# A planned hybrid decoder layer: buffers taken in the order of the plan, with slack in the plan, on one NeuronCore

## Chip, cores and metric

One NeuronCore of a Trainium2 chip runs the whole layer. The metric is the device time of one execution in microseconds (us). The engines are TensorE (PE, with its weight loads PEld), VectorE (DVE), ScalarE (ACT), GpSimd (POOL) and SyncE (SP), which issues most of the DMAs; ACT issues the others.

## What is computed

The input x is 1024 tokens by 1024 channels. One RMS norm, one combined projection, three groups of heads, a gate for each group, one output projection, the residual and a last RMS norm:

```python
h = rms_norm(x)
p = h @ w_in                                   # columns for three groups
# RWKV-7, 8 heads of 64: a state S (64x64 per head), token after token
sa = einsum(S, -kk_t)
S  = S * w_t + sa * (kk_t * a_t) + v_t * k_t   # decay, delta rule, new value
y  = einsum(S, r_t)
# sparse attention, 4 heads of 64: three branches, summed under gates
# memory attention, 4 heads of 64, into 256 memory tokens
out = rms_norm(x + concat(rwkv, nsa, mem) * silu(gates) @ w_out)
```

## The kernel before

**The work.** Every wide projection is made three times with 128x512 products: the weights are split in a high part `wh` (ACT, line 635) and a low part `wl` (POOL or DVE, line 636) of one loaded tile `wr` (line 640, one buffer), and the normed input in two such parts `H`. A weight tile costs 48 products `pa<-H,wh` and `pa<-H,wl` and is needed by nothing else.

**RWKV** goes by four pairs of heads (hp0 to hp3 here), and then by 16 chunks of 64 tokens. DVE, ACT and POOL make the factors of a pair, PE multiplies them (`pa<-A,NP`), DVE masks the results (line 1007) and SP stores them in DRAM (`st_d`, lines 1011 to 1014). Within each chunk a triangular matrix has to be inverted. That is done for two pairs of heads at once, which is why there are two of them: **inverse 0** after hp1 and **inverse 1** after hp3. Each one

- loads the 32x32 diagonal blocks from `st_d` in an array A (line 818),
- makes 31 steps on DVE, two instructions each (lines 826 and 827, shapes of 31, 60, 87, ... elements that grow and then shrink again),
- copies the result (ACT, line 829), stores it in `md` and `nd` (lines 830, 832), loads `st_d` over A (line 839), `nd` in `S` (line 841, issued by ACT) and `md` in A (line 844),
- makes the remaining off-diagonal blocks by 32x32 products on PE (`pa<-S,A`, `pa<-A,S`), copies them (line 859), and stores the inverse in `st_d` (line 861).

The chunks load their matrices from `st_d` (line 1446). They are a chain through the state: each waits for the one before (`ch<-T,C`, `ch<-xe,C`, and ACT's copy `xe<-ch` of line 1468, once per chunk). The projections of the memory and sparse groups, their attention and the output projection have no part in this chain, and fill PE between its links.

**What sets the order.** Nothing of the order is left to chance. The stages are generators, and `flow()` runs them in a written order. Then a planner, `ordered()`, reads all instructions, estimates how long each takes, finds the dependences, ranks each instruction by how much work hangs on it (`_backward`) and plays the program once through (`_forward`): whichever instruction of an engine is ready and has the highest rank goes next. This is repeated `ROUNDS` times with the last result as the start, the best plan is kept, and each engine's instructions are chained in its order.

**Buffers.** Tiles of one tag share a few buffers. In the kernel before, tiles were given to buffers when the instructions were written, so in the written order; the planner had to keep it, and a rule in `_edges` held it there: a tile's writers may not begin before the first user of the tile before it in its tag.

Of the kernel before, what the change touches and what calls it, by code (L numbers as in the profile page):

```python
# [131 lines left out]

def _access(x):

    a = x.bass_ap
    t = a.tensor
    p = tuple((int(s), int(c)) for s, c in a.ap)
    n = 1
    for s, c in p[1:]:
        n *= c  # L140
    if type(t).__name__ != "Tile":
        return None, None, "D", p, n
    if t.space == DRAM:
# [12 lines left out]
    p0, c0 = divmod(int(a.offset), row)
    w = 1 if a.dtype == BF else 2
    key = (c0, p[1:], w)
    if key not in _MASKS:
        idx = np.array([c0])  # L160
        for s, c in p[1:]:
            idx = np.unique((idx[:, None] + np.arange(c)[None, :] * s).ravel())
        _MASKS[key] = _bits((idx[:, None] * w + np.arange(w)[None, :]).ravel())
    return t, {q: _MASKS[key] for q in range(p0 // 32, (p0 + p[0][1] - 1) // 32 + 1)}, "S", p, n


def _times(o, ins, outs):

    i, kind = o.i, o.kind
    n = max([x[4] for x in ins + outs] or [1])  # L170
    psum = any(x[2] == "P" for x in ins)
    big = sum(x[4] > 1 for x in ins)
    o.lock = False
    if o.e == "Activation":
        few = sum(x[4] == 1 for x in ins) if n > 1 else 0
        o.took = 170 + 0.84 * n + 85 * (few > 0) + 110 * (len(outs) > 1)
        o.occ = o.took - 110
    elif o.e == "DVE":
        if kind == "InstMemset":
            o.took = 60 + 0.83 * n  # L180
        elif kind == "InstTensorCopy" and not psum:
            o.took = 150 + 0.53 * n
        elif getattr(i, "is_tensor_tensor_scan", False):
            o.took = 150 + 2.1 * n
        elif kind == "InstTensorScalarPtr" and big == 1 and not psum and not getattr(i, "is_scalar_tensor_tensor", False):
            o.took = 150 + 0.5 * n
        else:
            o.took = 145 + 1.045 * n
        if kind == "InstTensorScalarPtr" and n > 64 and sum(x[4] == 1 for x in ins):
            o.took += 60  # L190
        o.occ = max(60.0, o.took - 82)
        o.lock = not psum and (kind == "InstTensorTensor" or kind == "InstTensorCopy" or getattr(i, "is_scalar_tensor_tensor", False))
    else:
        if kind == "InstMemset":
            o.took = 98 + 0.83 * n
        elif kind == "InstTensorTensor" and i.op == OP.pow:
            o.took = 380 + 157 * n
        elif kind == "InstTensorTensor":
            o.took = 165 + 2.15 * n if n < 1000 else 2600.0
        else:  # L200
            o.took = 185 + 0.5 * n
        o.occ = o.took - 42 if n > 8 else o.took + 70
        o.lock = bool(ins)


def _matmul(i):
    mov, sta = i.ins[0].bass_ap, i.ins[1].bass_ap
    n = 1
    for s, c in tuple(mov.ap)[1:]:
        n *= c  # L210
    c = 1
    for s, q in tuple(sta.ap)[1:]:
        c *= q
    r = tuple(sta.ap)[0][1]
    kind = "r" if sta.dtype == F32R else "b" if sta.dtype == BF else "t" if i.is_transpose else "f"
# [25 lines left out]
    return {"r": 180 + 0.42 * s[3], "t": 195 + 0.84 * s[3], "b": 205 + 0.42 * s[3], "f": 255 + 0.84 * s[3]}[s[0]]  # L241


def _read(instructions):
    ops = []
    for k, i in enumerate(instructions):
        kind = type(i).__name__
        if kind in ("BassTilePoolBoundary", "InstTileManualSchedule"):
            continue
        o = Op()  # L250
        o.i, o.k, o.kind, o.e = i, len(ops), kind, str(i.engine).split(".")[-1]
        ins = [_access(x) for x in i.ins if hasattr(x, "bass_ap")]
        outs = [_access(x) for x in i.outs if hasattr(x, "bass_ap")]
        o.reads, o.writes = [x[:2] for x in ins if x[0] is not None], [x[:2] for x in outs if x[0] is not None]
        o.dma, o.lock, o.shape = None, False, None
        if kind == "InstDMACopy":
            run = 1 << 30
            for t, m, w, p, n in ins + outs:
                c = 1
                for s, q in reversed(p):  # L260
                    if s != c and q != 1:
                        break
                    c *= q
                run = min(run, 4 * c)
            n = 4 * ins[0][4] * ins[0][3][0][1]
            d = min(run, 8192)
            n = max(4 * outs[0][4] * outs[0][3][0][1], 4) / d
            load = outs[0][2] == "S"
            o.dma = (330 + max(0.0, n - 256) * 0.7, 1170.0 if load else 670.0, n * (9 + d * 0.0366) / 16, 720.0 if load else 450.0)
            o.took = sum(o.dma)  # L270
            o.occ = o.dma[0] + 50 if o.e == "SP" else 200.0
        elif o.e == "PE":
            o.shape = _matmul(i)
            o.occ, o.took = _step(o.shape), _done(o.shape)
        else:
            _times(o, ins, outs)
        ops.append(o)
    return ops


def _depend(ops):
# [62 lines left out]
    return took, late  # L344


def _edges(ops, users, tags, took):

    preds = [None] * len(ops)
    for o in ops:  # L350
        preds[o.k] = {p: 0 for p in o.data}
        for p in o.same:
            preds[o.k][p] = 1
    for names in tags.values():
        for a, b in zip(names, names[1:]):
            p = users[a][0]
            for k in users[b]:
                if k != p and any(w[0].name == b for w in ops[k].writes):
                    preds[k].setdefault(p, 2)
    for t, old in took.items():  # L360

        for k in users[t]:
            if any(w[0].name == t for w in ops[k].writes):
                for p in users[old]:
                    if p != k:
                        preds[k][p] = 1 if ops[k].e == "PE" and ops[p].e == "PE" else 0

    after, head = {}, list(range(len(ops)))
    for a, b in zip(ops, ops[1:]):
        if a.e == b.e == "PE" and _mode(a.shape) == _mode(b.shape) != (128, 128) and len(block(head, a.k, after)) < BLOCK:  # L370
            after[a.k] = b.k
            head[b.k] = head[a.k]
    for k in range(len(ops)):
        h = head[k]
        if h != k:
            for p, same in preds[k].items():
                if head[p] != h:
                    preds[h][p] = min(same, preds[h].get(p, 2))
    for o in ops:
        o.preds = preds[o.k]  # L380
    return preds, after
# [56 lines left out]
def _forward(ops, preds, after, rank, phase):  # L438
# [20 lines left out]
    while done < n:  # L459
# [73 lines left out]
    return order, start, end  # L533


MARGIN = 0.0
FIRST = 250
BLOCK = 32
SWITCH = 700.0
BUFS = {"A_a": N_A, "C_a": 2, "P4_p4": N_P4, "NP_p4": N_NP, "S2_s2": N_S2, "N2_s2": N_N2, "T2_s2": N_T2, "H_h": 2, "wr_w": N_WR,  # L540
        "wl_w": 2, "wh_w": 2, "pa_ps": 6, "ch_ps": 2, "ss_small": 2, "edge_small": 2, "n8_small": 2, "ost_small": 2, "mst_small": 4,
        "cst_small": 1, "st_small": 2, "wst_small": 3, "xe_small": 1, "sgc_small": 1, "md_dram": 2, "nd_dram": 2}
ROUNDS = 10


def ordered(nc, tc, log=None):
    ops = _read(list(nc.cur_bb.bb.instructions))
    _depend(ops)
    users, tags = _tiles(ops)
    seq = list(range(len(ops)))  # L550
    best, start = None, seq
    for n in range(ROUNDS):
        took, late = _slots(users, tags, seq)
        preds, after = _edges(ops, users, tags, took)
        rank = _backward(ops, preds, start)
        rank = [r + max(0.0, FIRST - k) * 1e3 for k, r in enumerate(rank)]
        order, start, end = _forward(ops, preds, after, rank, 1100.0)
        if log is not None:
            log(n, late, end)
        if best is None or end < best[0]:  # L560
            best = end, order
        seq = sorted(range(len(ops)), key=lambda k: (start[k], k))
    end, order = best
    for e, line in order.items():
        for a, b in zip(line, line[1:]):
            tc.add_manual_dep(ops[b].i, ops[a].i.name, mybir.DependencyInfo(mybir.DependencyClass.NoSync, mybir.DependencyReason.DATA), reason="order")


def build(tc, x, mem, w_in, w_gl, w_kv, w_out, lora, pv_d, rows_d, cst_d, rope_d, w1_d, pos_d, w2_d, out):
    nc = tc.nc  # L570
    V, S, G, PE = nc.vector, nc.scalar, nc.gpsimd, nc.tensor
    ctx = ExitStack()
    with ctx:
# [1224 lines left out]
        spawn(R_O, out_proj())  # L1798
        spawn(R_P, projections())
        flow()  # L1800
        ordered(nc, tc)

# [99 lines left out]
```

## Time and profile before

| quantity | value |
|---|---|
| median of three runs | 800.5 us (799.58 to 803.46) |
| profiled execution | 801.87 us |
| its span in the trace | 800.1 us |
| its mean granted TensorE clock | 0.968 of full speed |
| PE busy | 730.0 us, 91% of the span |
| DVE, ACT, POOL busy | 531.3, 387.8, 349.4 us |

The span is what the trace shows from the first instruction to the last; the execution has 1.8 us more. PE's share of busy time is a mean over stages, and its clock has two levels, 2.4 GHz (granted 1.0) and 1.2 GHz (granted 0.5); a granted clock between them is a mean over a stretch.

### The profile page before, as it was taken

To read this page: it belongs to the slowest core of one execution; us is meant where nothing else is said; L and a number is where in the kernel's file an instruction comes from. 1 tells how busy PE (TensorE), PEld (TensorE's weight loads), DVE (VectorE), ACT (ScalarE), POOL (GpSimd) and SP (SyncE) were. 2 spreads that over 40 slices of the span, in tenths; PEclk is the share of its full clock that TensorE was granted. 3 is DMA by queue.
4 is the path that set the end of the run, shared out by engine and by line. 5 is a ranking of instruction groups with operands and counts; after the bars stand their busy time and mean duration, and the time that the engine had idled before them with its cause. 6 is when DMAs were issued, how large, how long until landed. Compare 5 with 4: busy or idle time off the path is not lost. (4 is left out here: it accounts for less than half of the span.)

```text
span 800.1 us, 15116 instructions
## 1 busy us (share of the span) xinstructions
PE 730.0 (91%) x5738; PEld 599.8 (75%) x5738; DVE 531.3 (66%) x1044; ACT 387.8 (48%) x854; POOL 349.4 (44%) x370
## 2 busy tenths in 40 slices
PE   3889999999980899898999989999998999999996
PEld 3778888888870787686886767676777889888885
DVE  5843677488994449652679875938878767776432
ACT  5553344353532024323477744544477666665531
POOL 3535528264540013122445656655334054255674
PEclk9999999999995699898999999999999999999999
DMA  8111674756469873594755585532525020121121
GB/s 336 43 54 40 161 169 107 200 142 159 119 158 189 142 197 118 128 196 164 231 164 176 186 262 180 200 120 62 157 80 151 2 79 28 54 79 54 54 86 59
DMA packets 124744, 105.67 MB, mean 132 GB/s; under 512 B 50816, under 2 KB 108544, under 8 KB 122496
## 3 DMA queue, kind: packets, MB, share of 16 engines
q1 hardware_dynamic: 108096, 95.57, 42.7%
q10 hardware_dynamic: 16576, 9.14, 4.2%
q8 instruction: 45, 0.74, 0.4%
q14 instruction: 27, 0.22, 0.1%
HBM read 68.52 MB, written 36.18 MB: 131 GB/s over the span
## 5 line engine op out<-in xcount | busy, mean ns | idle before, releaser
L610 PE MATMUL pa<-H,wh 128*128 128x512 f32 (+1 forms) x928 | 292.2, 395 | 4.6 <-DVE H L705 2.9
L610 PEld LDWEIGHTS pa<-H,wh 128*128 128x128 f32 x928 | 170.9, 191 | 40.0 <-DVE H L705 4.0
L610 PE MATMUL pa<-H,wl 128*128 128x512 f32 (+1 forms) x464 | 181.1, 391 | 0.3 <-DVE wl L636 0.3
L636 POOL TENSOR_TENSOR wl<-wr,wh 128x1024 fp32r<-128x1024 f32 x27 | 68.0, 2518 | 88.3 <-ACT wh L635 71.5
L610 PEld LDWEIGHTS pa<-H,wl 128*128 128x128 f32 x464 | 88.0, 190 | 18.2 <-DVE wl L636 0.8
L610 PE MATMUL ch<-H,C 128*128 128x512 f32 x360 | 100.6, 407 | 0.0
L610 PE MATMUL pa<-A 128*128 128x256 f32 (+4 forms) x416 | 75.1, 306 | 2.5 <-DVE A L897 2.1
L635 ACT ACTIVATE wh<-wr 128x1024 fp32r<-128x1024 f32 x32 | 33.9, 1058 | 79.2 <-PE pa L610 72.8
L610 PEld LDWEIGHTS ch<-H,C 128*128 128x128 f32 x360 | 64.0, 189 | 10.0
L610 PEld LDWEIGHTS pa<-A 128*128 128x128 f32 (+1 forms) x416 | 51.1, 173 | 8.1 <-issue 2.5
L1171 DVE TENSOR_TENSOR N<-pa,S 128x512 fp32r<-128x512 f32 (+1 forms) x76 | 44.8, 613 | 17.8 <-ACT S L1170 15.2
L1596 DVE TENSOR_REDUCE wst<-pa 128x1 f32<-128x384 f32 (+3 forms) x96 | 46.6, 514 | 12.1 <-PE pa L610 11.7
L610 PEld LDWEIGHTS ch<-T,C 128*64 128x64 f32 (+1 forms) x1008 | 35.1, 139 | 22.1 <-ACT T L1483 5.7
L610 PE MATMUL ch<-T,C 128*64 128x64 f32 (+1 forms) x1008 | 42.1, 230 | 8.8 <-DMA C<-st_d 3.1
L1170 ACT ACTIVATE S<-pa 128x512 fp32r<-128x512 f32 (+1 forms) x76 | 38.5, 542 | 16.7 <-PE pa L1636 15.9
L1493 DVE SCALAR_TENSOR_TENSOR T<-ch,gc,sgc 64x64 f32<-64x64 f32 x120 | 33.9, 283 | 9.2 <-PE ch L610 5.5
L876 ACT ACTIVATE T<-pa,pv 128x512 f32<-128x512 f32 x34 | 23.1, 679 | 32.4 <-PE pa L610 28.3
L1606 ACT ACTIVATE NP<-pa,wst 128x384 f32<-128x384 f32 (+3 forms) x52 | 29.0, 565 | 17.6 <-DVE wst L1596 11.1
L1475 POOL TENSOR_TENSOR sgc<-T,gc 64x256 f32<-64x256 f32 x30 | 20.7, 689 | 36.2 <-DVE T L1493 34.9
L1677 POOL TENSOR_TENSOR S<-S,N 128x512 f32<-128x512 f32 x8 | 10.3, 1290 | 50.3 <-DVE N L1676 22.0
L610 PE MATMUL ch<-S,A 128*128 128x256 f32 x132 | 30.9, 298 | 0.8 <-ACT S L1170 0.8
L610 PE MATMUL ch<-N,A 128*128 128x256 f32 x132 | 30.4, 297 | 1.0 <-DVE N L1171 1.0
(273 smaller groups left out, 1498.3 us busy)
## 6 DMA issues: line engine op xcount, KB each, us to landing
C<-st_d SPq DMA_DIRECT2D x16, 1024.0 KB, 5.3
wr<-in_w_in_dram SPq DMA_DIRECT2D x28, 512.0 KB, 3.8
st_d<-C SPq DMA_DIRECT2D x32, 256.0 KB, 4.7
st_d<-A SPq DMA_DIRECT2D x24, 256.0 KB, 3.7
A<-in_x_dram SPq DMA_DIRECT2D x8, 512.0 KB, 7.8
st_d<-NP SPq DMA_DIRECT2D x8, 512.0 KB, 5.3
P<-in_x_dram SPq DMA_DIRECT2D x8, 512.0 KB, 3.5
out_dram<-P SPq DMA_DIRECT2D x7, 512.0 KB, 2.7
```

The costliest lines, as they stand in the source:

```text
L610: PE.matmul(o, l, r, start=start, stop=stop, skip_group_check=True, **k)
L635: S.activation(hi, src, AF.Copy)
L636: E.tensor_sub(lo, src, hi.bitcast(F32))
L876: S.activation(t[:, 4:516], o, AF.Identity, scale=col(C_MU + idx))
L1170: S.activation(th[:, 0:w], psum_t, AF.Copy)
L1171: V.tensor_sub(tl_[:, 0:w], psum_t, th[:, 0:w].bitcast(F32))
L1475: G.tensor_mul(sgc[r], sv[r, q], gcb[r])
L1493: V.scalar_tensor_tensor(svn[r, q, hp, :], pn[r, hp, :], g1[r, hp], sgc[r, hp, :], op0=OP.mult, op1=OP.add)
L1596: V.tensor_reduce(st[:, 3 + a, hh:hh + 1], sc[:, 0:cw], axis=AX.X, op=OP.max, negate=True)
L1606: S.activation(p[:, c0:c0 + cw], sc[:, 0:cw], AF.Exp, bias=m, accum_out=acc)
L1677: G.tensor_add(bo[0], bo[0], bo[1])
```

## The change

All engine calls go through `Queues`, which writes each call down with its arguments and issues nothing. The planner reads these records in place of instructions; its formulas for durations are the same, by other names. For each tag, tiles are now sorted by their first use in the last plan (`taken`), and `_slots` gives them to buffers in that order; the rule of `_edges` that held the written order is gone. At the end, all calls are issued in the order of their planned beginnings, so that the pools hand out buffers in the plan's order. Three numbers change too: `MARGIN`, which the planner adds to every dependence between engines, from 0 to 150 ns; `BLOCK`, the largest number of small products that it keeps together, from 32 to 16; and `ROUNDS` from 10 to 30. No instruction is added, removed or given another shape: 6,994 instructions stand on both sides, one for one, in other orders.

```diff
-    for names in tags.values():
-        for a, b in zip(names, names[1:]):
-            p = users[a][0]
-            for k in users[b]:
-                if k != p and any(w[0].name == b for w in ops[k].writes):
-                    preds[k].setdefault(p, 2)
...
+class Queue:
...
+    def __getattr__(self, f):
+        def call(*args, **kw):
+            o = Op()
+            o.k, o.e, o.name, o.args, o.kw, o.call = len(self.ops), self.name, f, args, kw, getattr(self.engine, f)
+            self.ops.append(o)
+        return call
...
-MARGIN = 0.0
+MARGIN = 150.0
 FIRST = 250
-BLOCK = 32
+BLOCK = 16
...
-ROUNDS = 10
...
+ROUNDS = 30
...
     for n in range(ROUNDS):
-        took, late = _slots(users, tags, seq)
-        preds, after = _edges(ops, users, tags, took)
+        at = {k: n for n, k in enumerate(seq)}
+        taken = {t: sorted(names, key=lambda x: min(at[k] for k in users[x])) for t, names in tags.items()}
+        took, late = _slots(users, taken, seq)
+        preds, after = _edges(ops, users, took)
...
+    last = {}
+    for k in best[1]:
+        o = ops[k]
+        i = o.call(*o.args, **o.kw).ins
+        if o.e in last:
+            tc.add_manual_dep(i, last[o.e], mybir.DependencyInfo(mybir.DependencyClass.NoSync, mybir.DependencyReason.DATA), reason="order")
+        last[o.e] = i.name
...
-    nc = tc.nc
+    nc = Queues(tc.nc)
```

What this does to the order is seen in the rows of both programs. In the changed program every row has line 574, the one that issues, so rows are known by their tiles.

**PE around inverse 0.** In the kernel before its products (array `A_1462`) come directly behind two groups of 128x128 products of hp3, and the last products of hp3 (`A_1986`) come behind it, among products with the projection weights:

```order
L610 MATMUL pa_2185<-H_143,wl_2181 128x512
L1004 MATMUL ch_2434<-cst_81,NP_2216 128x128 x4
L1004 MATMUL ch_2461<-cst_81,NP_2216 128x128 x4
L610 MATMUL pa_2228<-S2_2128,A_1462 32x32 x32
L610 MATMUL pa_2322<-S2_2137,A_1462 32x32 x32
...
L610 MATMUL pa_2377<-H_143,wl_2181 128x512
...
L610 MATMUL pa_2424<-A_1986,NP_2216 128x128
...
L610 MATMUL pa_2452<-A_1986,NP_2216 128x128
```

In the changed program the array of inverse 0 is `A_336` and hp3's factors are `A_419`:

```order
L574 MATMUL pa_465<-A_419,NP_455 128x128
...
L574 MATMUL pa_469<-A_419,NP_455 128x128
...
L574 MATMUL pa_520<-H_105,wh_517 128x512
L574 MATMUL pa_459<-S2_439,A_336 32x32 x32
L574 MATMUL pa_529<-A_508,wh_528 128x256
L574 MATMUL pa_518<-H_104,wl_516 128x512
...
L574 MATMUL pa_457<-S2_438,A_336 32x32 x32
```

Inverse 0's products have moved behind the last products of hp3, and between the two now stand 137 rows, nearly all of them 128x512 products with weights. In all, 248 instructions that stood behind inverse 0's first product stand ahead of it now, 216 of them such 128x512 products. In the same way 117 have moved ahead of inverse 1's first product and 128 ahead of chunk 0's.

**DVE at the end of inverse 0.** Before, its last steps (`A_1462`) are done 18 rows ahead of the first step of inverse 1 (`A_2503`):

```order
L827 TENSOR_TENSOR A_1462<-A_1462,P4_1602 128x30x2
L826 TENSOR_TENSOR P4_1602<-A_1462 128x31
L827 TENSOR_TENSOR A_1462<-A_1462,P4_1602 128x31
...
L1007 TENSOR_TENSOR C_2210<-pa_2452,maskb_136 128x512
...
L826 TENSOR_TENSOR P4_2603<-A_2503 128x31
L827 TENSOR_TENSOR A_2503<-A_2503,P4_2603 128x31
```

In the changed program (`A_336` is inverse 0, `A_480` inverse 1):

```order
L574 TENSOR_TENSOR P4_360<-A_336 128x192
L574 TENSOR_TENSOR wl_516<-wr_515,wh_517 128x1024
L574 TENSOR_TENSOR P4_491<-A_480 128x31
L574 TENSOR_TENSOR A_336<-A_336,P4_360 128x24x8
...
L574 TENSOR_TENSOR P4_360<-A_336 128x60
L574 TENSOR_TENSOR A_480<-A_480,P4_491 128x7x25
L574 TENSOR_TENSOR A_336<-A_336,P4_360 128x30x2
L574 TENSOR_TENSOR P4_491<-A_480 128x192
L574 TENSOR_TENSOR P4_360<-A_336 128x31
L574 TENSOR_TENSOR A_480<-A_480,P4_491 128x8x24
L574 TENSOR_TENSOR A_336<-A_336,P4_360 128x31
```

The first step of inverse 1 now stands ahead of the last 15 instructions of inverse 0, and the two go on in turns: 15 of inverse 0, 16 of inverse 1 and four others from `P4_491 128x31` to the last `A_336 128x31`.

**SP behind the two inverses.** In the changed program the queue from the stores of inverse 0 on reads as follows (`wr` are weight loads, `md`, `nd` and `st_d` as above):

```order
L574 DMA md_334<-A_336 128x1024
L574 DMA nd_335<-A_336 32x1024 x2
L574 DMA A_336<-st_d_108 64x16x64 x3
L574 DMA wr_533<-in_w_in_dram 128x1024
L574 DMA A_336<-st_d_108 64x16x64
L574 DMA A_336<-md_334 32x16x32 x8
L574 DMA wr_540<-in_w_kv_dram 128x1024
...
L574 DMA A_480<-st_d_108 64x16x64 x4
L574 DMA wr_570<-in_w_kv_dram 128x1024
L574 DMA A_480<-md_478 32x16x32 x8
```

Before, inverse 0's transfers had no weight load among them, and inverse 1's had one:

```order
L830 DMA md_1460<-A_1462 128x1024
L832 DMA nd_1461<-A_1462 32x1024 x2
L839 DMA A_1462<-st_d_147 64x16x64 x4
L1050 DMA g_d_150<-T2_2170 128x512
L844 DMA A_1462<-md_1460 32x16x32 x8
...
L839 DMA A_2503<-st_d_147 64x16x64 x3
L640 DMA wr_3160<-in_w_kv_dram 128x1024
L839 DMA A_2503<-st_d_147 64x16x64
```

From the stores of inverse 0 to the first load of chunk 0, six weight loads stand in the changed queue: `wr_533`, `wr_540`, `wr_545`, `wr_559`, `wr_570`, `wr_586`.

## Rows read from the trace of the kernel before

**Rows 1.** The page: busy time of the engines, and TensorE's granted clock by slices.
```profile
PE 730.0 (91%) x5738; PEld 599.8 (75%) x5738; DVE 531.3 (66%) x1044; ACT 387.8 (48%) x854; POOL 349.4 (44%) x370
PEclk9999999999995699898999999999999999999999
```

**Rows 2.** Stretches: length, busy time and instructions of each engine, PE's granted clock, DMA share.
```profile
200.00:240.00 40.00, 37.66 (x207) 31.21 (x205) 39.13 (x66) 17.69 (x28) 20.21 (x20) 0.96 0.55 138
240.00:280.00 40.00, 18.45 (x319) 15.48 (x320) 17.93 (x37) 4.97 (x7) 0.47 (x3) 0.62 0.87 165
280.00:380.00 100.00, 91.15 (x735) 75.02 (x734) 55.78 (x117) 32.96 (x53) 23.13 (x22) 0.93 0.63 161
380.00:520.00 140.00, 133.44 (x1599) 102.30 (x1600) 108.56 (x256) 85.19 (x213) 80.57 (x89) 1.00 0.63 200
...
280.00:300.00 20.00, 20.00 (x90) 16.55 (x89) 8.41 (x20) 5.22 (x7) 2.86 (x4) 1.00 0.74 197
320.00:340.00 20.00, 16.69 (x76) 13.82 (x75) 13.26 (x34) 6.46 (x10) 3.33 (x3) 0.83 0.59 128
...
360.00:380.00 20.00, 16.08 (x156) 12.76 (x155) 4.65 (x12) 6.19 (x11) 5.91 (x4) 0.83 0.49 164
```

**Rows 3.** Timeline of PE around inverse 0: start, length, instruction, count, wait before it.
```profile
239.06 0.39 PE L610 MATMUL pa<-H,wl 128*128 128x512 f32 x1
242.35 1.06 PE L1004 MATMUL ch<-cst,NP 128*128 128x128 f32 x8 [2.90 <-DVE NP L984]
260.21 0.28 PE L610 MATMUL pa<-S,A 32*32 32x32 f32 x2 [16.80 <-DMA A<-st_d]
262.89 3.59 PE L610 MATMUL pa<-S,A 32*32 32x32 f32 x126 [2.40 <-DMA S<-nd]
...
274.74 1.16 PE L610 MATMUL pa<-A,NP 64*128 64x128 f32 x16
...
277.79 0.40 PE L610 MATMUL pa<-H,wl 128*128 128x512 f32 x1
278.11 1.16 PE L610 MATMUL pa<-A,NP 64*128 64x128 f32 x16
```

**Rows 4.** Timeline of DVE and SP's queue (SPq) ahead of inverse 0's products.
```profile
247.63 0.20 DVE L826 TENSOR_TENSOR P<-A 128x31 f32<-128x31 f32 x1
247.87 0.21 DVE L827 TENSOR_TENSOR A<-A,P 128x31 f32<-128x31 f32 x1
248.12 1.93 ACT L829 ACTIVATE A<-A 128x1024 f32<-128x1024 f32 x1 [4.01 <-DVE A L827]
...
253.74 3.97 SPq L839 DMA_DIRECT2D A<-st_d  x4
...
260.02 4.46 SPq L844 DMA_DIRECT2D A<-md  x5
```

**Rows 5.** Timeline from hp3's masks to inverse 1's first step on DVE.
```profile
279.31 1.29 DVE L1007 TENSOR_TENSOR C<-pa,maskb 128x512 f32<-128x512 f32 x2 [2.08 <-PE pa L610]
...
287.24 1.15 SPq L818 DMA_DIRECT2D A<-st_d  x2
...
294.91 0.19 DVE L826 TENSOR_TENSOR P<-A 128x31 f32<-128x31 f32 x1 [5.64 <-DMA A<-st_d]
```

**Rows 6.** Lines 827, 859 and 1468: instructions, shortest, median and longest ns, first and last start.
```profile
L827 DVE TENSOR_TENSOR A<-A,P x62: 183/363/2503, 179.1 to 330.1; 128x31 f32<-128x31 f32 x4, 128x60 f32<-128x60 f32 x4, 128x87 f32<-128x87 f32 x4, 128x112 f32<-128x112 f32 x4
...
L859 DVE COPY A<-pa x8: 679/684/691, 269.1 to 353.2; 32x512 f32<-32x512 f32 x8
...
L1468 ACT ACTIVATE xe<-ch x16: 573/597/606, 369.1 to 518.9; 128x512 f32<-128x512 f32 x16
```

**Rows 7.** Timeline of PE: first products of inverse 1 and of chunk 0.
```profile
343.01 1.20 PE L610 MATMUL pa<-S,A 32*32 32x32 f32 x64
...
367.06 1.98 PE L610 MATMUL ch<-T,C 128*64 128x64 f32 x32 [3.06 <-DMA C<-st_d]
```

**Rows 8.** The page: a weight tile's load (KB, us to landing), its split on ACT and POOL.
```profile
L636 POOL TENSOR_TENSOR wl<-wr,wh 128x1024 fp32r<-128x1024 f32 x27 | 68.0, 2518 | 88.3 <-ACT wh L635 71.5
...
L635 ACT ACTIVATE wh<-wr 128x1024 fp32r<-128x1024 f32 x32 | 33.9, 1058 | 79.2 <-PE pa L610 72.8
...
wr<-in_w_in_dram SPq DMA_DIRECT2D x28, 512.0 KB, 3.8
```

More of the change, by code (lines that the diff above doesn't have):

```diff
@@ L133, in _access @@
 def _access(x):
-    a = x.bass_ap
-    t = a.tensor
+    a, t = x, x.tensor
     p = tuple((int(s), int(c)) for s, c in a.ap)
@@ L167, in _times @@
 def _times(o, ins, outs):
-    i, kind = o.i, o.kind
+    f = o.name
     n = max([x[4] for x in ins + outs] or [1])
@@ L172, in _times @@
     big = sum(x[4] > 1 for x in ins)
+    one = sum(x[4] == 1 for x in ins)
     o.lock = False
     if o.e == "Activation":
-        few = sum(x[4] == 1 for x in ins) if n > 1 else 0
-        o.took = 170 + 0.84 * n + 85 * (few > 0) + 110 * (len(outs) > 1)
+        o.took = 170 + 0.84 * n + 85 * (one > 0 and n > 1) + 110 * (len(outs) > 1)
         o.occ = o.took - 110
     elif o.e == "DVE":
-        if kind == "InstMemset":
+        if f == "memset":
             o.took = 60 + 0.83 * n
-        elif kind == "InstTensorCopy" and not psum:
+        elif f == "tensor_copy" and not psum:
             o.took = 150 + 0.53 * n
-        elif getattr(i, "is_tensor_tensor_scan", False):
+        elif f == "tensor_tensor_scan":
             o.took = 150 + 2.1 * n
-        elif kind == "InstTensorScalarPtr" and big == 1 and not psum and not getattr(i, "is_scalar_tensor_tensor", False):
+        elif f == "tensor_scalar" and big == 1 and not psum:
             o.took = 150 + 0.5 * n
@@ L188, in _times @@
             o.took = 145 + 1.045 * n
-        if kind == "InstTensorScalarPtr" and n > 64 and sum(x[4] == 1 for x in ins):
+        if f in ("tensor_scalar", "scalar_tensor_tensor") and n > 64 and one:
             o.took += 60
         o.occ = max(60.0, o.took - 82)
-        o.lock = not psum and (kind == "InstTensorTensor" or kind == "InstTensorCopy" or getattr(i, "is_scalar_tensor_tensor", False))
+        o.lock = not psum and f in ("tensor_tensor", "tensor_mul", "tensor_sub", "tensor_add", "tensor_copy", "scalar_tensor_tensor", "tensor_tensor_scan")
     else:
-        if kind == "InstMemset":
+        if f == "memset":
             o.took = 98 + 0.83 * n
-        elif kind == "InstTensorTensor" and i.op == OP.pow:
+        elif o.kw.get("op") == OP.pow:
             o.took = 380 + 157 * n
-        elif kind == "InstTensorTensor":
+        elif f in ("tensor_mul", "tensor_sub", "tensor_add", "tensor_tensor"):
             o.took = 165 + 2.15 * n if n < 1000 else 2600.0
@@ L203, in _times, with _matmul @@
         o.lock = bool(ins)
-def _matmul(i):
-    mov, sta = i.ins[0].bass_ap, i.ins[1].bass_ap
+def _matmul(sta, mov, transposed):
     n = 1
@@ L241, in _done, with __init__, _read @@
     return {"r": 180 + 0.42 * s[3], "t": 195 + 0.84 * s[3], "b": 205 + 0.42 * s[3], "f": 255 + 0.84 * s[3]}[s[0]]
[L244 to L253, printed above, removed]
+class Queue:
+    def __init__(self, engine, name, ops):
+        self.engine, self.name, self.ops = engine, name, ops
+    def __getattr__(self, f):
[4 more added lines that the diff above has]
+        return call
+class Queues:
+    def __init__(self, nc):
+        self.ops = []
+        for n, e in (("vector", "DVE"), ("scalar", "Activation"), ("gpsimd", "Pool"), ("tensor", "PE"), ("sync", "SP")):
+            setattr(self, n, Queue(getattr(nc, n), e, self.ops))
+def _read(ops):
+    isap = lambda x: hasattr(x, "tensor") and hasattr(x, "ap")
+    for o in ops:
+        outs = [_access(x) for x in list(o.args[:1]) + [o.kw.get("accum_out")] if isap(x)]
+        ins = [_access(x) for x in list(o.args[1:]) + [v for k, v in o.kw.items() if k != "accum_out"] if isap(x)]
         o.reads, o.writes = [x[:2] for x in ins if x[0] is not None], [x[:2] for x in outs if x[0] is not None]
         o.dma, o.lock, o.shape = None, False, None
-        if kind == "InstDMACopy":
+        if o.name == "dma_start":
             run = 1 << 30
@@ L272, in _read @@
         elif o.e == "PE":
-            o.shape = _matmul(i)
+            o.shape = _matmul(o.args[2], o.args[1], True) if o.name == "transpose" else _matmul(o.args[1], o.args[2], False)
             o.occ, o.took = _step(o.shape), _done(o.shape)
@@ L344, in _slots, with _edges @@
     return took, late
-def _edges(ops, users, tags, took):
+def _edges(ops, users, took):
     preds = [None] * len(ops)
@@ L542, with ordered @@
         "cst_small": 1, "st_small": 2, "wst_small": 3, "xe_small": 1, "sgc_small": 1, "md_dram": 2, "nd_dram": 2}
-ROUNDS = 10
-def ordered(nc, tc, log=None):
-    ops = _read(list(nc.cur_bb.bb.instructions))
+ROUNDS = 30
+def ordered(tc, ops, log=None):
+    _read(ops)
     _depend(ops)
@@ L559, in ordered @@
             log(n, late, end)
+        seq = sorted(range(len(ops)), key=lambda k: (start[k], k))
         if best is None or end < best[0]:
[L561 to L566, printed above, removed]
+            best = end, seq
+    last = {}
[5 more added lines that the diff above has]
+        last[o.e] = i.name
 def build(tc, x, mem, w_in, w_gl, w_kv, w_out, lora, pv_d, rows_d, cst_d, rope_d, w1_d, pos_d, w2_d, out):
-    nc = tc.nc
+    nc = Queues(tc.nc)
     V, S, G, PE = nc.vector, nc.scalar, nc.gpsimd, nc.tensor
@@ L1800, in build @@
         flow()
-        ordered(nc, tc)
+        ordered(tc, nc.ops)
 W_OFF_NSA, W_OFF_MEM = 2176, 3084
```

4 lines of the change are left out of this document (1 added, 3 removed).

## The prediction

> **What bounds the kernel now.** I read the page first. PE is busy for 730.0 of 800.1 us and its clock is at full speed in every slice but a few in the middle [rows 1]. So PE's work sets the time, and what can be won without less work is PE's idle time and its time at half clock. The table of stretches says where both lie [rows 2]. From 280 to 300 us PE did 90 products 128x512 without a gap: 20.00 / 90 = 0.222 us each, the price of a wide product below. From 240 to 280 it is busy for 18.45 of 40 us at a mean clock of 0.62.
>
> The timeline of PE shows the hole [rows 3]. After 239.06 no product with weights stands ahead of inverse 0 any more; eight products of hp3 follow, and then PE waits 16.80 us for a load of `A<-st_d` and soon 2.40 us for `S<-nd`. It is a wait by order: the products that run from 280 to 300 need nothing of inverse 0. The chain behind the wait is DVE's last step at 247.87, ACT's copy, the stores and two rounds of loads [rows 4]: from the end of that step (248.08) to the first product at 260.21 it takes 12.1 us.
>
> What PE loses from 200 to 380 us, where the orders differ most, is this. Idle: 2.3 + 21.6 + 8.9 = 32.8 us [rows 2]. Half clock: a mean of 0.62 over 40 us is about 30 us at half, from the wait until 274; PE worked for about 11.5 of them (260.2 to 274 less 2.4), which at full clock would have taken half, so 5.7 are lost. By the same reading 0.83 over 20 us is 6.8 us at half, 3.4 lost, twice, and 0.96 over 40 us loses 1.6. Together 14.1, so **46.9 us** in all.
>
> **The change, step by step.** Writing calls down costs the device nothing: the instructions are the same, and what follows is order alone.
>
> *Inverse 0.* The products of inverse 0 now stand behind hp3's last ones, with 137 rows between: 134 wide products (29.7 us) and three groups of four 128x128, at half of 1.06 us each [rows 3], so 31.3 us of cover. What PE waits for is a chain that starts with those same hp3 products, because inverse 1's first step stands ahead of inverse 0's last 15 on DVE, and DVE takes them in order:
> - hp3's last product ends at 279.27 [rows 3]; masks, stores and loads, and inverse 1's first step comes at 294.91 [rows 5]: 15.6 us, of which 14.3 lie behind the mask;
> - then 31 steps in turns and four others. Two steps of 31 elements begin 0.24 us apart [rows 4]; the median of all steps of line 827 is 0.363 [rows 6], and these are of the shorter half; the others take 1.29 / 2 = 0.65 [rows 5]. Bounds: 31 x 0.24 + 2.6 = 10.0 and 31 x 0.363 + 2.6 = 13.9. I take 11.6, nearer the lower one, since shapes run from 31 to 192 elements;
> - then 12.1 us as now.
>
> The sum is 39.3, less the cover of 31.3: PE still **waits 8.0 us**, and behind it works at half clock for a while: 3.4 lost, as in either of the stretches with 0.83. Of the work moved ahead, some 21 us stand ahead of hp3's last products, so PE comes to these at about 239.5 + 21 = 260 us rather than 274, or some 3 us sooner if the half clock before 240 goes too; inverse 0's first product is then at 257 to 260 + 39.3, so about 298.
>
> For the load of inverse 1's blocks the profile gives 14.3 us from mask to step [rows 5], for four stores and four loads in one queue with others between. The Trainium skill (DMA: Bandwidth & Descriptors, sections on the anatomy of one DMA and on latency) puts the fixed cost of a transfer at about 2 us, most of it the receipt of the write, a fit for the path by GpSimd; a store and a load would then be some 4 us, an estimate from that page. By it PE's wait is gone and the time about 764; by the row it is 775. The row is of this queue, so I go by it.
>
> *Inverse 1.* Its steps took from 294.91 to 330.3, 35.4 us with DVE's other work [rows 5, 6]; with inverse 0's 15 among them (about 4.4 us) they end near 275 + 40 = 315, and 12.7 us later (330.3 to 343.01 [rows 6, 7]) the products are ready, at 328. PE's work from inverse 0's first product to inverse 1's was 82.8 us less idle (2.4 and 5.8) and half clock (9.1), so 65.5; 52.6 us have left it (216 wide products at 0.222 and 32 smaller ones), 19.2 have come (117 instructions at their durations): 32. PE is there at 298 + 32 + 3.4 = 333. **No wait**, with 5 us to spare.
>
> *Chunk 0.* From inverse 1's first product to chunk 0's it is now 24.05 us [rows 7], 13.2 of them from the last copy's end at 353.9 [rows 6]: copies, stores, the load of `C`. Nothing in that chain is shortened. So chunk 0 begins at about 357 in place of 367, the wait of 3.06 and the half clock (3.4) behind it stay.
>
> Kept of the 46.9: 8.0 + 3.4 + 3.1 + 3.4, and half of the 3.9 lost between 200 and 240, in sum 19.9. **Gain 27.0.**
>
> *The chunks.* 16 chunks take 149.8 us from the first copy to the last, 9.99 each [rows 6]; PE is 95% busy [rows 2]. Work worth 18.6 us (128 instructions) now stands ahead of chunk 0 and 13.0 of it still ahead of chunk 15, so 5.6 us of filler are missing within. If PE sets the pace, the chunks take that much less; if the chain does, PE idles for it. Bounds 0 and +5.6; I take **+2.8**.
>
> *Blocks of 16, margin, rounds.* A passage between shapes costs what lies between 277.79 + 0.222 and 278.11 [rows 3], 0.1 us; there are 179 in place of 188: **-0.9**. The margin puts no instruction in the program; it can only choose orders with less tight hand-overs. All PE's idle time from 380 to 520 is 6.6 us [rows 2], and half of that either way bounds it: -3 to +3, taken as 0, hidden by the products between. The last 240 us of PE's work keep almost the same order: 0.
>
> Sum, against the profiled execution: 801.9 - 27.0 + 2.8 - 0.9 = 776.8. The median of the runs stands 1.4 below that execution, which makes 775.4: **775 us** is forecast. With the bounds of the DVE steps (10.0 to 13.9, which move the wait as they are), of the chunks and of the margin the likeliest case lies between 768 and 785.
>
> **The rivals.**
> 1. *The hole closes.* If the loads for inverse 1 come some 8 us sooner than in rows 5, PE finds inverse 0 done: 8.0 + 3.4 less, 764; with chunk 0's wait gone too, 758. For it: the 14.3 us hold several stores and loads of one queue, with a weight load among them. Against it: the other two such chains took 12.1 and 13.2 us, so this length is the rule here.
> 2. *The stall comes back elsewhere.* DVE stands still for 5.64 us before inverse 1's first step [rows 5]. Now the rest of inverse 0 queues behind that instruction, so every us that the loads come later is a us on PE. Loads 8 us later (more traffic now lies in that queue) and a chain-bound chunk loop (+2.8) give 775 + 10.8 = 786; 785 to 796.
> 3. *Slower: weight loads behind waiting transfers.* SP takes its queue in order. From inverse 0's stores to the loads of `md` it was held for 12 us [rows 4], and there now stand six weight loads from there to chunk 0. A tile takes 3.8 + 1.06 + 2.52 = 7.4 us to load and split [rows 8], its 48 products 10.7, so 3.3 us of lateness are free with one `wr` buffer; a load that is late by the full 12 costs 8.7. Six cost 52, which gives 828; from four on (35 us) the gain is gone and the kernel slower. Against it: before, inverse 1 had such a load amid its transfers too, and PE's whole idle time from 280 to 380 was 8.9 us.
> 4. *No change*: only if rivals 2 and 3 happen to take the whole gain, 797 to 804.
>
> **How the numbers follow.** Likeliest case (hole partly closed, 768 to 785) 0.54; rival 1 (757 to 767) 0.20; rival 2 (785 to 796) 0.13; no change 0.05; rival 3 0.08. The half per cent that a measurement of this kernel can tell is 4 us, so faster means below 796.5: 0.54 + 0.20 + 0.13 = 0.87, same 0.05, slower 0.08. The range of 759 to 795 leaves out the last two cases and the edges of the first two rivals.
>
> **What would show it.** Right: PE busy without a gap from 200 to about 288 us; then one wait of some 8 us before a `pa<-S,A` 32x32, named DVE or a DMA behind inverse 0's last step; inverse 1's first step on DVE at 273 to 276 with a DMA wait before it; no wait before inverse 1's products; the first `xe<-ch` near 359 and the last at 503 to 509. Wrong: no wait at inverse 0 (rival 1), a wait above 15 us there (rival 2), waits of PE that name `wh` or `wl` between 250 and 380 (rival 3), or 16 copies `xe` that span much more than 150 us, which would mean that the new buffers hold up the chunks.

## The result and the profile after

The changed kernel takes 781.4 us (779.59 to 783.57, four runs) beside 801.4 us of the kernel before on the same chip: a ratio of 0.9751, with a 95% interval of 0.9715 to 0.9787. The forecast was 775 us in a range of 759 to 795. The profiled execution took 783.57 us with a span of 781.8, so 18.3 us less span than before.

The page of the changed kernel, its rows for the engines and for the granted clock, to be read beside [rows 1]:

```profile
PE 728.4 (93%) x5736; PEld 596.8 (76%) x5738; DVE 540.4 (69%) x1044; ACT 389.5 (50%) x854; POOL 342.6 (44%) x370
PEclk9999999999999998979999999999999999999998
```

PE has the same work in a shorter span, and the stretch at low clock in the middle has shrunk. The stretches answer to [rows 2] (columns as there):

```profile
200.00:240.00 40.00, 39.75 (x243) 33.15 (x242) 31.44 (x44) 21.49 (x34) 23.52 (x23) 1.00 0.61 154
240.00:280.00 40.00, 40.00 (x206) 32.85 (x205) 35.38 (x77) 12.54 (x19) 4.03 (x7) 1.00 0.73 193
280.00:380.00 100.00, 87.67 (x989) 72.03 (x988) 61.52 (x121) 38.30 (x79) 18.50 (x15) 0.91 0.78 182
380.00:520.00 140.00, 131.16 (x1673) 98.86 (x1672) 103.46 (x244) 78.20 (x185) 83.80 (x93) 1.00 0.59 183
...
280.00:300.00 20.00, 18.07 (x192) 15.44 (x190) 14.61 (x31) 4.63 (x4) 5.27 (x4) 0.83 1.01 165
300.00:320.00 20.00, 18.38 (x216) 14.91 (x209) 15.16 (x24) 7.04 (x12) 7.26 (x7) 1.00 0.54 138
320.00:340.00 20.00, 13.06 (x77) 10.87 (x76) 13.15 (x31) 11.73 (x29) 2.35 (x1) 0.93 0.69 165
340.00:360.00 20.00, 19.90 (x330) 17.03 (x330) 8.80 (x15) 4.54 (x10) 2.39 (x1) 0.81 0.89 152
```

From 240 to 280 us, where PE had been busy for 18.45 us, it is now busy for all 40, at full clock. From 200 to 380 it is idle for 0.25 + 12.3 = 12.6 us (32.8 before), and the clocks of 0.83, 0.93 and 0.81 cost 3.4 + 1.4 + 3.8 = 8.6 (14.1 before): 21.2 us lost in place of 46.9. Of the idle time that is left, 1.6 + 6.9 = 8.5 us lie between 300 and 340; of the half clock, most lies from 280 to 300 and from 340 to 360.

PE's timeline around inverse 0, beside [rows 3] (all rows of this kernel have line 574):

```profile
254.11 1.16 PE L574 MATMUL pa<-A,NP 64*128 64x128 f32 x16
...
257.25 1.16 PE L574 MATMUL pa<-A,NP 64*128 64x128 f32 x16
...
290.40 0.22 PE L574 MATMUL pa<-S,A 32*32 32x32 f32 x2
292.54 1.62 PE L574 MATMUL pa<-S,A 32*32 32x32 f32 x62 [1.93 <-DMA S<-nd]
...
342.59 1.92 PE L574 MATMUL pa<-S,A 32*32 32x32 f32 x64
```

hp3's last products now end at 258.41 (279.27 before), and products with weights run on from there to 290.40, where inverse 0's first products begin without a wait; 1.93 us are waited for `S<-nd` just behind. The row at 342.59 is inverse 1's first. The chain that has to fit in the 32 us up to 290.40, on DVE:

```profile
259.68 0.68 DVE L574 TENSOR_TENSOR C<-pa,maskb 128x512 f32<-128x512 f32 x1
...
273.01 0.19 DVE L574 TENSOR_TENSOR P<-A 128x31 f32<-128x31 f32 x1 [3.14 <-DMA A<-st_d]
...
280.94 0.47 DVE L574 TENSOR_TENSOR A<-A,P 128x192 f32<-128x192 f32 x2
```

The first row is the last of hp3's masks. Inverse 1's first step waits for its load at 273.01, as forecast; the third row holds inverse 0's last step, which ends at 281.41.

The costliest waits of PE by line and what ended them (us in total, times, longest):

```profile
PE pa L574 <- DVE A L574: 16.5, 4, 13.7
PE pa L574 <- DVE S L574: 4.6, 6, 1.5
PE pa L574 <- ACT wh L574: 3.9, 3, 2.3
PE pa L574 <- POOL wl L574: 3.0, 2, 1.7
```

The one long wait (13.7) is the start of the program. The others are short; the timeline of PE between 314 and 340 has most of those for weights:

```profile
316.18 0.50 PE L574 MATMUL pa<-H,wh 128*128 128x512 f32 x1 [0.35 <-ACT wh L574]
...
318.82 0.50 PE L574 MATMUL pa<-H,wl 128*128 128x512 f32 x1 [1.27 <-POOL wl L574]
...
323.39 0.36 PE L574 MATMUL pa<-A 128*128 128x256 f32 x1 [1.33 <-DVE A L574]
...
330.81 1.00 PE L574 MATMUL pa<-cst,NP 128*128 128x128 f32 x4 [1.14 <-ACT NP L574]
...
336.02 0.50 PE L574 MATMUL pa<-A,wh 128*128 128x256 f32 x2 [2.30 <-ACT wh L574]
...
338.45 0.58 PE L574 MATMUL pa<-A,wl 128*128 128x256 f32 x1 [1.69 <-POOL wl L574]
```

Four of the six are for `wh` or `wl`. The two longest, 2.30 and 1.69, belong to one weight tile. Its load on SP and its split on ACT:

```profile
319.69 0.52 SPq L574 DMA_DIRECT2D wr<-in_w_kv_dram  x1
...
332.38 2.03 ACT L574 ACTIVATE A<-A 128x1024 f32<-128x1024 f32 x1
...
334.92 1.05 ACT L574 ACTIVATE wh<-wr 128x1024 fp32r<-128x1024 f32 x1
```

The load was issued 15 us ahead of the split, and the split waits for no load: it stands in ACT's order behind the copy of inverse 1's result (332.38). The copies of the chunks, in the view of [rows 6]:

```profile
L574 ACT ACTIVATE xe<-ch x16: 597/598/600, 369.6 to 511.9; 128x512 f32<-128x512 f32 x16
```

The last step of inverse 1 in the timeline of DVE:

```profile
331.75 0.22 DVE L574 TENSOR_TENSOR A<-A,P 128x31 f32<-128x31 f32 x1
```

The chunks begin at 369.6, no sooner than before (369.1), and last 142.3 us in place of 149.8. From their first copy to the end of the span it was 431.0 us and is 412.2. So the whole gain lies behind that first copy: work that used to be done there stands ahead of it now. That the chunks don't begin earlier goes back to inverse 1: its 62 instructions on DVE (31 steps of two; "62 steps" below) take from 273.0 to 332.0, 59 us where they took 35.4. It begins 22 us sooner and ends 1.7 us later. The experiments test this link.

### The profile page after: what moved, and what is told of

Read it like the earlier page. It is cut to its first block, busy times and chain, and to the rows that moved or that the text cites. A ratio compares the mean times of both kernels' runs of the same rounds, so it can differ in the third digit from the quotient of the medians.

```text
span 781.8 us, 15135 instructions
## 1 busy us (share of the span) xinstructions
PE 728.4 (93%) x5736; PEld 596.8 (76%) x5738; DVE 540.4 (69%) x1044; ACT 389.5 (50%) x854; POOL 342.6 (44%) x370
## 4 chain that ended last, share of the span: by engine, by line
PE 67%; DVE 12%; DMA 11%; ACT 3%; POOL 3%; issue 2%; SPq 0%; ACTq 0%; DVEq 0%; POOLq 0%
PE pa L574 47%; PE ch L574 20%; DVE A L574 4%; DVE T L574 2%; DMA A<-in_x_dram 2%; DMA yd<-S 2%; DVE S L574 1%; DVE P L574 1%; DVE wst L574 1%; DMA st_d<-A 1%; DMA S<-nd 1%; DMA C<-st_d 1%; DVE N L574 1%; DMA S<-g_d 1%; DMA wr<-in_w_out_dram 1%
## 5 line engine op out<-in xcount | busy, mean ns | idle before, releaser
L574 POOL TENSOR_TENSOR wl<-wr,wh 128x1024 fp32r<-128x1024 f32 x27 | 66.1, 2447 | 104.6 <-ACT wh L574 96.2
L574 PE MATMUL ch<-H,C 128*128 128x512 f32 x360 | 104.4, 408 | 0.6 <-POOL H L574 0.4
L574 ACT ACTIVATE S<-pa 128x512 fp32r<-128x512 f32 (+4 forms) x112 | 58.5, 544 | 44.6 <-PE pa L574 32.6
L574 PE MATMUL pa<-A 64*64 64x64 f32 (+4 forms) x416 | 74.6, 307 | 2.5 <-DVE A L574 1.7
L574 PE MATMUL ch<-T,C 128*64 128x64 f32 (+1 forms) x1008 | 39.4, 226 | 5.0 <-ACT T L574 1.5
L574 DVE SCALAR_TENSOR_TENSOR T<-ch,gc,sgc 64x64 f32<-64x64 f32 x120 | 33.9, 283 | 13.1 <-PE ch L574 6.1
L574 ACT ACTIVATE T<-pa,pv 128x512 f32<-128x512 f32 x34 | 23.1, 681 | 34.3 <-PE pa L574 23.7
L574 PE MATMUL pa<-cst,NP 128*128 128x128 f32 x212 | 33.6, 278 | 3.2 <-ACT NP L574 1.5
L574 PEld LDWEIGHTS pa<-cst,NP 128*128 128x128 f32 x212 | 25.7, 142 | 9.6 <-ACT NP L574 2.8
```

The source lines that it names most:

```text
L574: i = o.call(*o.args, **o.kw).ins
```

## The experiments

**What brings the gain.** The change has two parts, the order of the buffers and three numbers. Each alone:

```diff
# numbers_only, from the kernel before
-MARGIN = 0.0
+MARGIN = 150.0
-BLOCK = 32
+BLOCK = 16
-ROUNDS = 10
+ROUNDS = 30
# buffers_only, from the changed kernel: these three lines the other way
```

> The kernel before with the three numbers of the change alone (margin 150 ns, blocks of 16, 30 rounds) and buffers still in the written order. Theory A, the order of buffers is what held the work back: the wait before inverse 0's products stays at 14 us or more and the time at 797 to 805 us. Theory B, the margin and the longer search bring the gain: 780 to 790 us and a wait below 8 us.

> The changed kernel with the three old numbers (margin 0, blocks of 32, 10 rounds): buffers in the plan's order alone. Theory A: at least three quarters of the gain, 778 to 787 us, no wait above 5 us before inverse 0's products, since some 160 rows that stood behind them stand ahead. Theory B: 794 to 802 us.

The numbers alone: ratio 1.007 (1.0038 to 1.0102). The hole is there:

```profile
245.03 1.94 PE L1004 MATMUL ch<-cst,NP 128*128 128x128 f32 x8 [8.70 <-DVE NP L984]
258.02 0.28 PE L610 MATMUL pa<-S,A 32*32 32x32 f32 x2 [11.05 <-DMA A<-st_d]
```

The wait before inverse 0 is 11.05, under the 14 that was expected, with another 8.70 in front of it, and the time of 806.9 us is 2 above the range of theory A. The buffers alone: 774.5 us, ratio 0.9658 (0.9596 to 0.972), below the range of A and 0.9% below the whole change; these two intervals just touch. Theory A holds in what it says of the cause: the gain comes from the order of the buffers. The three numbers bring none, and probably give some of it back. PE's waits at inverse 0 there are 2.90 and 2.47 us:

```profile
274.41 0.31 PE L574 MATMUL pa<-S,A 32*32 32x32 f32 x2 [2.90 <-DMA S<-nd]
277.19 1.88 PE L574 MATMUL pa<-S,A 32*32 32x32 f32 x62 [2.47 <-DMA A<-st_d]
```

**Which buffers.** The old rule was put back for the tags of a condition `KEEP`, which are then also taken in the written order:

```diff
+KEEP = lambda tag: tag.startswith("pa")          # keep_pa; free_pa: not ...
...
+    for tag, names in tags.items():
+        if not KEEP(tag):
+            continue
+        for a, b in zip(names, names[1:]):
+            p = users[a][0]
...
-        taken = {t: sorted(names, key=lambda x: min(at[k] for k in users[x])) for t, names in tags.items()}
+        taken = {t: names if KEEP(t) else sorted(names, key=lambda x: min(at[k] for k in users[x])) for t, names in tags.items()}
```

> The changed kernel, in which only the tiles of one tag, the PSUM banks pa, are taken in the written order under the old rule; all other tags in the plan's order. If these banks are what closed the way for the products with weights (theory A1): the wait before inverse 0's products is back at 14 us or more, the time at 793 to 803. If the SBUF arrays are what held them (A2): 778 to 786, no such wait.

> The reverse: only the PSUM banks pa in the plan's order, all other tags in the written order under the old rule. A1: no wait above 5 us before inverse 0's products, 780 to 789. A2: the wait stays, 793 to 803.

With only the PSUM banks held to the written order the time is 812.1 us, above A1's range too, the ratio 1.0119 (1.0071 to 1.0166), and the hole is larger than before:

```profile
272.09 0.28 PE L583 MATMUL pa<-S,A 32*32 32x32 f32 x2 [23.24 <-DMA S<-nd]
```

So these banks suffice to make the hole: by the old rule a product with weights may not begin in a bank before inverse 0's product, whose tile is ahead of its own in the written order, has begun. But freeing them alone gains nothing: 808.8 us, 1.0075 (1.0043 to 1.0107). The wait ahead of inverse 0 is gone, as A1 said:

```profile
269.15 2.47 PE L583 MATMUL pa<-S,A 32*32 32x32 f32 x128
```

The time that was to follow from it did not come; inverse 1's first step comes at 295.9 and the chunks' first copy at 387.8, 18.7 us later than before. Which of the other arrays keeps hp3 and inverse 1 back there was not tried. Both programs write the calls down and issue them as the changed kernel does, so that alone is not where the gain comes from.

**What gives part of it back.** One number at a time, from the changed kernel:

```diff
# margin0
-MARGIN = 150.0
+MARGIN = 0.0
# block32
-BLOCK = 16
+BLOCK = 32
# margin300
-MARGIN = 150.0
+MARGIN = 300.0
# margin_cross: the margin only where the engines differ
-            d = 0.0 if same == 2 else q.occ if same else q.took + LAG[o.e] + MARGIN
+            d = 0.0 if same == 2 else q.occ if same else q.took + LAG[o.e] + MARGIN * (q.e != o.e)
...
-            ready[x] = max(ready[x], s if same == 2 else free[e] if same else f + LAG[ops[x].e] + MARGIN)
+            ready[x] = max(ready[x], s if same == 2 else free[e] if same else f + LAG[ops[x].e] + MARGIN * (ops[x].e != e))
```

The last one rests on something that the code shows and the section on the change says too narrowly: the planner leaves the margin out between two PE instructions and adds it to nearly every other dependence, so also to the 61 that join the 62 steps of one inverse on DVE.

> The changed kernel with margin 0 (blocks of 16, 30 rounds). Buffers alone gave 774.5 us and the change 781.4, so one of the three numbers gives some 7 us back. T1, the margin that is added between two instructions of one engine spreads the inverses' steps on DVE: 772 to 777, inverse 1's 62 steps within 50 us. T2, blocks of 16: 779 to 784. T3, the margin between engines: 772 to 777.

> The changed kernel with blocks of 32 in place of 16. T1 and T3: still 779 to 784, with inverse 1's steps spread over more than 55 us. T2: 772 to 777.

> The changed kernel with a margin of 300 ns, twice as much. T1 and T3: the loss grows, 785 to 795; by T1 inverse 1's 62 steps are spread over more than 60 us (59 in the changed kernel, 48 with buffers alone). T2, or a margin that helps on the chip: 775 to 784.

> The changed kernel with the margin of 150 ns added only where the two instructions are on different engines. T1: 772 to 777, inverse 0's and inverse 1's steps no longer in turns. T2 and T3: 779 to 784.

Then the margin between the steps by itself, added to the kernel with buffers alone, and taken out of the changed kernel:

```diff
                 V.tensor_add(mt[:, 0:n, s + 1:], mt[:, 0:n, s + 1:], t3)
+                for o in nc.ops[-2:]:
+                    o.loose = True               # tight_steps: o.tight
...
-... + MARGIN
+... + 150.0 * (hasattr(o, 'loose') and hasattr(q, 'loose'))
# tight_steps: MARGIN * (not (hasattr(o, 'tight') and hasattr(q, 'tight')))
```

> Buffers alone (margin 0, blocks of 32, 10 rounds: 774.5 us, the 62 steps of inverse 1 within 47.9 us), but with a margin of 150 ns between two DVE steps of the same inverse. T1, this margin makes the planner put other work between the steps: spread of 54 to 60 us as in the changed kernel (59), 779 to 785. T3, the margin between engines is what costs: 772 to 777.

> The reverse: the changed kernel with its margin of 150 ns everywhere but between two DVE steps of one inverse. T1: spread below 51 us, and 772 to 778 if inverse 1 begins near 272 as before. T3: 779 to 786. T4, what the search happens to find weighs more than either: inverse 1 begins near 300, as with the margin between engines alone, and the time is 795 to 802.

All programs together. "First step" and "steps" are the beginning of inverse 1 on DVE and the time to the end of its last step; "first copy" is that of the chunks, and "rest" the span less it. Times in us, ratios against the kernel before on the same chip:

| program | ratio (95%) | first step | steps | first copy | rest |
|---|---|---|---|---|---|
| before | 1 | 294.9 | 35.4 | 369.1 | 431.0 |
| numbers_only | 1.0070 (1.0038 to 1.0102) | 289.0 | 43.5 | 371.1 | 431.6 |
| keep_pa | 1.0119 (1.0071 to 1.0166) | 301.2 | 40.7 | 382.1 | 427.3 |
| free_pa | 1.0075 (1.0043 to 1.0107) | 295.9 | 51.2 | 387.8 | 417.2 |
| changed kernel | 0.9751 (0.9715 to 0.9787) | 273.0 | 59.0 | 369.6 | 412.2 |
| buffers_only | 0.9658 (0.9596 to 0.9720) | 271.5 | 47.9 | 358.4 | 412.8 |
| margin0 | 0.9717 (0.9662 to 0.9773) | 271.2 | 45.3 | 356.3 | 418.2 |
| block32 | 0.9723 (0.9681 to 0.9764) | 272.4 | 53.6 | 363.8 | 415.6 |
| margin300 | 0.9847 (0.9776 to 0.9918) | 263.9 | 69.8 | 373.1 | 413.8 |
| margin_cross | 0.9997 (0.9975 to 1.0018) | 300.5 | 49.8 | 387.0 | 412.2 |
| loose_steps | 0.9811 (0.9763 to 0.9859) | 273.8 | 65.0 | 376.2 | 409.5 |
| tight_steps | 0.9808 (0.9760 to 0.9856) | 292.7 | 47.9 | 377.6 | 408.9 |
| hot01 | 0.9851 (0.9802 to 0.9900) | 291.1 | 35.5 | 366.4 | 422.6 |
| late_chunk0 | 0.9820 (0.9764 to 0.9876) | 285.8 | 38.0 | 376.4 | 409.9 |

The margin between steps spreads them, as T1 said: with all buffers in the plan's order the steps take 53.6 to 69.8 us in the four programs that have it, most with 300 ns, and at most 49.8 in the six that have not. Between the first and the last step DVE runs 99 to 129 instructions in the four and 75 to 88 in the six, so the margin lets other work in. Putting it on the steps alone cost 1.5% (0.9658 to 0.9811), more than T1's 779 to 785 (788.1 measured, with steps over 65.0 us for T1's 54 to 60), and against T3's no change. There PE waits long ahead of inverse 1's products:

```profile
PE pa L574 <- DMA S<-nd: 17.6, 2, 16.2
```

But T1 didn't hold the other way round: without the margin between steps (tight_steps, margin_cross) the steps are short and inverse 1 begins 20 to 27 us later, and these are slower than the changed kernel. T4 comes nearest there, in kind and not in its numbers (292.7 and 788.0 us in tight_steps, for 300 and 795 to 802): what the search finds moves by more than the term in question. margin_cross, at 799.5 us, missed all three theories: the margin between engines alone costs 2.8% beside margin0 on the same chip, more than the whole margin does. block32 missed both of its theories by a little (777.6 us, steps over 53.6), margin0 is at the edge of T1 and T3 (777.6), and margin300 (789.8) went as T1 said. So the spread of the steps is shown to come from the margin between them. What it costs in time is shown by loose_steps alone, in one plan. Which number gives back the 0.9% in the changed kernel is not shown: margin0 and block32 are both 2 to 3 us under it by their ratios, within the intervals.

The table shows one link that holds in every program. The first copy comes 36.7 to 40.7 us behind the end of inverse 1's steps (first step plus steps) in all but late_chunk0, so it is that end, and not inverse 1's beginning, that goes with the beginning of the chunks.

margin_cross shows what the late beginning looks like; DVE stands still for 11.94 us in front of inverse 1's first step:

```profile
300.45 2.30 DVE L574 TENSOR_TENSOR P<-A 128x31 f32<-128x31 f32 x1 [11.94 <-DMA A<-st_d]
```

**Does the beginning of the chunks set the end?** Two more, from the kernel with buffers alone: the inverses first on every engine, and chunk 0's load by one more DRAM array.

```diff
# hot01: every operation of inverse() is marked hot
+        rank = [r + 1e6 * getattr(o, 'hot', False) for r, o in zip(rank, ops)]
# late_chunk0
-            nc.sync.dma_start(ct, st_d[:, n])
+            if n == 0:
+                late = dr.tile([128, 4, 4, 128], F32, name="late")
+                nc.sync.dma_start(late, st_d[:, n])
+                nc.sync.dma_start(ct, late)
+            else:
+                nc.sync.dma_start(ct, st_d[:, n])
```

> Buffers alone, and everything of both inverses goes first on its engine as soon as it is ready. In eight programs so far the span ended 412 to 418 us after the first copy xe of the chunks wherever the PSUM banks are free. U1, the beginning of the chunks sets the end: first copy before 355, and the span 412 to 418 after it, so below 771. U2, PE's work sets the end: 772 to 778 whatever the first copy.

> Buffers alone, with the load of chunk 0 taken through one more DRAM array: one store and one load more in the chain before chunk 0, no work on any compute engine. U1: the first copy comes 5 to 9 us later (363 to 367) and the time rises by as much, 778 to 784. U2: 772 to 777, since PE has other work ready.

The copies of hot01:

```profile
L575 ACT ACTIVATE xe<-ch x16: 570/600/626, 366.4 to 509.3; 128x512 f32<-128x512 f32 x16
```

And those of late_chunk0:

```profile
L574 ACT ACTIVATE xe<-ch x16: 592/598/602, 376.4 to 509.5; 128x512 f32<-128x512 f32 x16
```

late_chunk0 went as U1 said in kind: later chunks and a later end, by 18.0 and 15.1 us of the profiles where 5 to 9 were expected. It's not a clean test, since the search also began inverse 1 14 us later; but it ended only 4.4 us later, and from that end to the first copy it took 52.6 us in place of 39.0. So the way through one more array cost 13.6 us of the 18.0 by itself, more than the 5 to 9. hot01 missed both: its chunks didn't begin early, since inverse 1 began at 291.1, and its time is 791.5 us with a rest of 422.6. Of the ten programs with all buffers in the plan's order nine have a rest of 408.9 to 418.2, while the first copy ranges over 30.7 us. So in these the end goes with the first copy, though not us for us: from margin0 to the changed kernel the first copy moves by 13.3 and the span by 7.3. hot01 shows that it isn't the only thing that counts.

## Why the prediction was right, and by how much its steps were off

**The hole is a wait by order, and closes: right.** It fits the two runs above: the old order of one tag of buffers makes it, and with all of them free it's gone. 46.9 us were counted as lost from 200 to 380 and 19.9 as kept; measured are 21.2 kept. The gain of that stretch was forecast at 27.0 and is 25.7. That these two are so close is luck in part, because two errors cancel: from 280 to 300 us, around inverse 0, 1.9 idle and 3.4 of half clock were lost where 11.4 were forecast, and from 300 to 380 15.6 where 6.5 were.

**Inverse 0's wait was over-sized.** hp3's last product to inverse 1's first step: 15.6 forecast, 273.01 - 258.41 = 14.6 measured; the steps in turns: 11.6 and 8.4, below the lower bound of 10.0; last step to first product: 12.1 and at most 290.40 - 281.41 = 9.0. In sum at most 32.0 for 39.3, and the cover of 31.3 was right (32.0). So the wait of 8.0 shrank to the 1.93 for `S<-nd`. That is rival 1's outcome at this place, but not its reason: the loads for inverse 1 came about 1 us sooner and not 8, and most of the rest came from the steps in turns (3.2) and from the way behind them (3.1 or more). The half clock behind it (3.4) came as in the likeliest case. The other side of the weighing with the Trainium skill (DMA: Bandwidth & Descriptors, on the anatomy of one DMA and on latency) isn't what closed it: from the end of the last mask (260.36) to the first step the way took 12.7 us where the row had 14.3, near the row's and not near some 4 us that its fixed cost of 2 us gave as an estimate.

**Inverse 1 was under-sized.** Its steps were put at 40 us and take 59.0. Its products begin at 342.59 for 333, without a wait, as forecast, because PE had been held by other waits, 8.4 us in sum between 314 and 340 (one of 0.35 isn't shown above), 5.6 of them for `wh` and `wl`. These waits are the sign that was named for rival 3, at a fraction of its price, and in the main not by its mechanism: 4.0 of the 5.6 us were waited for a split that ACT did late, with its load issued long before. The first copy was forecast near 359 and came at 369.6; that is the step that failed. The margin was said to "only choose orders with less tight hand-overs" and was bounded at 3 us; that it also lies between two steps on one engine, and spreads them, was not seen. The 40 us added only inverse 0's 15 instructions to the old 35.4. From the first to the last step DVE did this in the changed kernel and before (length, busy time, instructions):

```profile
273.01:331.97 58.96, 46.38 (x107) 0.94 0.69 149
294.91:330.31 35.40, 33.33 (x77) 1.00 0.32 105
```

So there are 30 more instructions, 13.1 us of work, and DVE stands still for 12.6 us where it was 2.1.

**The rest.** Of the 25.7 us, 18.3 arrived. The last stretches of the changed kernel:

```profile
520.00:640.00 120.00, 112.69 (x770) 91.35 (x772) 98.59 (x196) 76.23 (x188) 48.32 (x42) 0.99 0.29 92
640.00:781.80 141.80, 134.77 (x834) 115.65 (x832) 79.45 (x179) 75.71 (x215) 72.23 (x79) 0.99 0.17 58
```

The same two of the kernel before, the second to its own end:

```profile
520.00:640.00 120.00, 113.90 (x882) 91.63 (x879) 88.99 (x174) 72.13 (x168) 45.91 (x36) 1.00 0.32 95
640.00:800.10 160.10, 153.02 (x952) 131.32 (x950) 91.79 (x210) 85.93 (x248) 83.80 (x92) 0.99 0.18 62
```

With 380 to 520, PE's idle time behind 380 us is 8.8 + 7.3 + 7.0 = 23.1 us for 6.6 + 6.1 + 7.1 = 19.8 before: 3.3 more, where 2.8 were put down for the chunks. The other 4 us are busy time: 728.4 us with 8.6 of half clock from 200 to 380, where it was 730.0 with 14.1. The clock of 0.99 behind 520 explains about one of them. The other three, where fewer passages between shapes were to save 0.9, stay open. In time they weigh most: the sum forecast 27.0 - 2.8 + 0.9 = 25.1 us less, 18.3 came, and some 5 of the 6.8 between these two are busy time (3.9 more for 0.9 less).

## What to carry to other kernels

Where a planner may reorder work but buffers are handed out in written order, look for the tag whose next tile has its first user behind a long wait: there PE had work and no bank. Here that tag alone took the wait away and gained nothing; all tags together gained. A slack in the plan is an order, too: added within one engine, it puts other work between the steps of the very chain that is late. And one plan isn't a measurement of a rule: small changes of the planner moved the changed kernel's time by up to 2.5%, so a part of a change is judged by the row that it should move (here the steps' spread and the chunks' first copy) and not by the total alone.

## What the hardware showed that was not expected

Two instructions on DVE that take 0.42 and 0.69 us elsewhere took 2.23 and 2.89 us beside a split of weights on GpSimd, and ended 0.3 and 0.6 us behind it. The two splits in the changed kernel's timeline:

```profile
295.67 2.38 POOL L574 TENSOR_TENSOR wl<-wr,wh 128x1024 fp32r<-128x1024 f32 x1 [8.19 <-PE pa L574]
...
304.32 2.47 POOL L574 TENSOR_TENSOR wl<-wr,wh 128x1024 fp32r<-128x1024 f32 x1 [6.28 <-ACT wh L574]
```

The instructions of DVE that began just behind them, between an undisturbed step (294.92) and an undisturbed instruction of the second one's shape (309.18):

```profile
294.92 0.42 DVE L574 TENSOR_TENSOR P<-A 128x255 f32<-128x255 f32 x1
...
296.10 2.23 DVE L574 TENSOR_TENSOR A<-A,P 128x255 f32<-128x255 f32 x1
...
304.45 2.89 DVE L574 SCALAR_TENSOR_TENSOR T<-S,T 128x512 f32<-128x512 f32 x1
...
309.18 0.69 DVE L574 SCALAR_TENSOR_TENSOR T<-S,T 128x512 f32<-128x512 f32 x1
```

The splits end at 298.05 and 306.79, the two on DVE at 298.33 and 307.34. The Trainium skill (SBUF — State Buffer, section "SBUF: two separate sides") says that DVE and GpSimd share one pair of ports, and that, where a DVE instruction has two inputs in SBUF and the GpSimd instruction reads SBUF, whichever begins second is blocked for the whole instruction of the other; these rows agree, with 2.23 us for a step that takes 0.42.
